# Four token tiles per PSUM bank in the opening of a transformer block, and a weight sum formed from another operand

## The chip, the cores and the metric

The kernel runs on one core of a Trainium2 chip. The metric is the device time of one execution in microseconds. A core has five engines that run side by side, each with its own queue in order: TensorE (PE, matrix products; the loading of its weights is shown as PEld), VectorE (DVE), ScalarE (ACT), GpSimd (POOL) and SyncE (SP, which here only issues transfers). The engines work on SBUF, a memory of 128 partitions. TensorE writes to PSUM, eight banks of 128 x 512 float32 numbers; VectorE and ScalarE read them from there.

## The reference: what is computed

One encoder block over 1024 tokens of width 1024, all in float32:

```python
h = layer_norm(x, ln_in_g, ln_in_b)
proj = h @ w_in[l]                       # 1024 x 11776: q, k, v of three attention groups, HGRN2 inputs, gates
att = dilated_attention(aq, ak, av, slopes)
rec = hgrn2(hq, hf_fwd, hf_bwd, hi, hg, lower_bounds[:, l], hgrn_norm_g[l])
merged = sigmoid(ga) * (att @ w_att_up[l]) + sigmoid(gh) * (rec @ w_hgrn_up[l])
h = layer_norm(ALPHA * h + merged @ w_o[l], ln1_g[l], ln1_b[l])
gate, up = split(h @ w_ffn_in[l], 2)
h = layer_norm(ALPHA * h + (silu(gate) * up) @ w_ffn_out[l], ln2_g[l], ln2_b[l])
```

The change touches the first two lines: the layer norm of `x`, and the way in which `h` and `w_in` are brought into the form in which the large product reads them.

## The kernel before

**Three products for one.** Every float32 operand is split into a high part, rounded to the format `float32r` that TensorE multiplies, and a low part, the rest (`split`, lines 212 and 220: a cast on ScalarE, a subtraction on GpSimd or VectorE). `mm3` (lines 268 to 270) then issues high times high, high times low, and low times high.

**Seven block products instead of eight.** The projection is done by a Strassen-Winograd scheme. The tokens are halved (512 and 512), the 1024 features are halved (512 and 512), and the columns of `w_in` are taken in pairs of tiles of 128. So the transposed activations form four blocks of 512 features by 512 tokens: b11 and b21 (first 512 tokens, lower and upper features) and b12 and b22 (second 512 tokens). From them come t1 = b12 - b11, t2 = b22 - t1, t3 = b22 - b12, t4 = b21 - t2. The seven products read b11, b21, t1, t2, t3, b22 and t4. On the weights' side stand a11, a12, a21, a22 and the sums s1 = a21 + a22, s2 = s1 - a11, s3 = a11 - a21, s4 = a12 - s2.

**The order of products.** `stream` is a generator. It takes two pairs of column tiles (g = 0 and 1) for each group n, and within a group the products in the order 1 (b11), 2 (b21), 6 (t2), 5 (t1), 7 (t3), 3 (b22), 4 (t4), each for both g. For the first two groups products 1 and 2 come ahead of everything else, so that TensorE has work that needs only b11 and b21. One product is four feature blocks of 128, three matmuls each: 12 matmuls of 128 x 512. The weight sums (`sums`, lines 605 to 607 and 610) are emitted five products ahead, the splits of the weights three ahead.

**The opening.** `phase0` makes the seven activation blocks, and calls `run()` to let `stream` emit one more step in between. For each of eight token tiles (128 tokens) it loads `x`, takes mean and variance on VectorE (`stats`, 336 and 340) with three small GpSimd operations (341 to 343), normalises in place on ScalarE in two halves (`norm`, 347), and transposes 128 x 128 squares on TensorE into a PSUM bank with tag `sd` (`transposed`, line 300). In a bank lie four feature blocks of one token tile. Since the gain `g` and the offset `b` of the layer norm differ from feature to feature and features are partitions after the transpose, each 128 x 128 square is evicted by an operation of its own with its own scalars (310 on ScalarE, 312 on VectorE). Tiles 0 to 3 give b11 and b21; tiles 4 to 7 give b12 and b22, and per tile t1 (422), t2 (426), t3 (428, GpSimd) and t4 (429), each 128 x 512 and split by `put`.

**What sets the order.** The program text gives priorities; a planner lays out each engine's queue by them and by its own estimate of when operands are there. Manual dependencies fix the rest: `ordered` chains operations with one key, `behind` puts an operation after a named one. Loads of `x` and of the weights share one chain on SP. There are four PSUM banks with the tag `sd`; the transposes of the opening and the accumulators of product 2 of the first two groups use them.

Of the kernel before, what the change touches and what calls it, by code (L numbers as in the profile page):

```python
# [10 lines left out]
F32 = mybir.dt.float32  # L11
# [68 lines left out]
class Block:  # L80
# [129 lines left out]
    def split(self, hi, lo, src, eng_hi="act", eng_lo="pool", key=None):  # L210
        nc = self.nc
        ins = nc.scalar.copy(hi, src) if eng_hi == "act" else nc.vector.tensor_copy(hi, src)  # L212
        if key == "x":
            self.ordered("xhi", ins)
        elif key == "w":
            self.behind(ins, self.gates.pop(0))
            key = None
# [75 lines left out]
    def transposed(self, pool, n, q, g, b, v=None, bufs=2, on_act=(1, 3, 6), two=False, gate=None):  # L293
# [3 lines left out]
        pa = self.ps_sd() if two else ps  # L297
        for k in range(4):
            p = pa if 4 * q + k in on_act else ps
            ins = nc.tensor.transpose(p[:, 128 * k:128 * (k + 1)], n[:, 128 * (4 * q + k):128 * (4 * q + k + 1)],  # L300
                                      self.ident)
            if gate:
                self.behind(ins, gate)
        if v is None:
            v = pool.tile([128, 4, 128], F32, name="tsv", tag="tsv", bufs=bufs)
        for k in range(4):
            kk = 4 * q + k
            p = (pa if kk in on_act else ps)[:, 128 * k:128 * (k + 1)]
# [5 lines left out]

    def phase0(self, pool, work):


        nc = self.nc
        xs, v, at = [], {}, {}

        def hold(n):
            t = pool.tile([128, D], F32, name=n, tag="xt", bufs=6)
            return t, [t[:, HALF * i:HALF * (i + 1)].rearrange("p (k c) -> p k c", k=4) for i in range(2)]

        def load(n):
            for _ in range(n):
                tt = len(xs)
                xs.append(hold("xt"))
                for h in range(2 if tt == 0 else 1):
                    s = slice(HALF * h, HALF * (h + 1)) if tt == 0 else slice(0, D)  # L330
                    self.queued(xs[tt][0][:, s], self.x[128 * tt:128 * (tt + 1), s])

        def stats(tt):
            st = self.tiny.tile([128, 2, 6], F32, name="bn0", tag="bnst", bufs=3)
            for j in range(2):
                ins = nc.vector.bn_stats(st[:, j, :], xs[tt][0][:, HALF * j:HALF * (j + 1)])
                if tt > 3:
                    self.behind(ins, at["lo", 3, "b11" if tt < 6 else "b21"])
            mv = self.mv0[:, tt, :]
            nc.vector.bn_aggr(mv[:, 0:2], st)  # L340
# [4 lines left out]
        def norm(tt, q):  # L345
            x, mv = xs[tt][0][:, HALF * q:HALF * (q + 1)], self.mv0[:, tt, :]
            ins = nc.scalar.activation(x, x, AF.Identity, bias=mv[:, 3:4], scale=mv[:, 2:3])
            at["norm", tt, q] = ins.ins.name
            if tt > 5:
                self.behind(ins, at["hi", tt - 2, "t2"])  # L350
            elif (tt, q) == (3, 1):
                self.behind(ins, at["hi", 3, "b11"])

        def put(tt, name, src, lo="dve"):
            c = slice(128 * (tt % 4), 128 * (tt % 4) + 128)
            hi, low = self.xb[name]
            ins = self.split(hi[:, :, c], low[:, :, c], src, eng_lo=lo, key="x" if tt > 3 else None)
            at["hi", tt, name], at["lo", tt, name] = self.cast, ins.ins.name
            return ins

        def turn(tt, q, dst, act, gate=None):
            gc, bc = self.col["gin"], self.col["bin"]
            return self.transposed(pool, xs[tt][0], q, gc, bc, dst, on_act=[4 * q + k for k in act], two=len(act) == 2,
                                   gate=gate)

        ACT, DVE = range(4), ()
# [5 lines left out]
        def late(tt, i):  # L372
            put(tt, ("t1", "t3", "b22", "t4")[i], v[tt][i])

# [3 lines left out]
        run(2)  # L378
        load(2)
        run()  # L380
        for tt in range(4):
            v[tt] = self.half3("v11"), self.half3("v21") if tt == 0 else                 pool.tile([128, 4, 128], F32, name=f"v21{tt}")
# [3 lines left out]
        norm(0, 0)  # L386
        norm(0, 1)
        turn(0, 0, v[0][0], DVE)
        stats(1)
        put(0, "b11", v[0][0], "pool")  # L390
        norm(1, 0)
        stats(2)
        turn(1, 0, v[1][0], ACT)
        norm(2, 0)
        put(1, "b11", v[1][0])
        stats(3)
        turn(2, 0, v[2][0], DVE)
        put(2, "b11", v[2][0])
        norm(3, 0)
        turn(3, 0, v[3][0], (2, 3))  # L400
        put(3, "b11", v[3][0])
        self.gates = [at["hi", 1, "b11"]] * 2 + [at["hi", 3, "b11"]] * 2
        run(2)
        for tt in range(4):
            if tt < 3:
                norm(tt + 1, 1)
            turn(tt, 1, v[tt][1], DVE if tt % 2 else ACT, self.product)
            self.left(put(tt, "b21", v[tt][1]))
            if tt == 1:
                load(2)  # L410
                run()
                stats(4)
        self.rest()
        run(3)
        for tt in range(4, 8):
            b11, b21 = v[tt - 4]
            norm(tt, 0)
            norm(tt, 1)
            t1, t2 = xs[tt][1]
            _, (b12, b22) = hold("vt")  # L420
            turn(tt, 0, b12, DVE if tt % 2 else ACT)
            nc.vector.tensor_sub(t1, b12, b11)
            if tt < 7:
                stats(tt + 1)
            turn(tt, 1, b22, ACT if tt % 2 else DVE)
# [1424 lines left out]
```

## Time and profile before

| | us |
|---|---|
| median of three runs | 2102.98 (2100.78 to 2104.03) |
| profiled execution, its time | 2102.44 |
| profiled execution, span of the trace | 2100.6 |
| TensorE busy in the span | 2025.1 |
| VectorE busy | 1380.4 |
| GpSimd busy | 1093.8 |
| ScalarE busy | 931.8 |

The profile shows one execution. Times in a timeline count from the start of the span. In a group of instructions `out<-in` names the tiles that are written and read; behind the first bar stand the busy time of the group in us and the mean of one in ns, behind the second the idle time of the engine ahead of the group and what ended it. `x4` says that the row stands for four instructions. In a row of waits stand the time in total, the number of waits and the longest one. The time of an execution is 1.84 us more than the span of its trace.

### The profile page before, as it was taken

The numbers are of one execution on the slowest core, as the hardware profiler recorded it, in microseconds if no ns is written. First come the engines' busy times: TensorE is split into PE (matmuls) and PEld (weight loads), VectorE is DVE, ScalarE is ACT, GpSimd is POOL, SyncE is SP. The second block draws the span as 40 slices with busy tenths as digits, with TensorE's granted clock in tenths as the row PEclk, the third lists the DMA queues.
The fourth block names the chain that finished last, engine by engine and source line by source line (L and its number), as shares of the span: only waits on it lengthen the run. The fifth ranks groups of instructions, "written<-read, shape, count | busy, mean of one in ns | idle before, by whom it ended". The sixth has DMA issues, their size and how long they took to land.

```text
span 2100.6 us, 30922 instructions
## 1 busy us (share of the span) xinstructions
PE 2025.1 (96%) x10974; PEld 1675.0 (80%) x10974; DVE 1380.4 (66%) x2158; ACT 931.8 (44%) x1878; POOL 1093.8 (52%) x903
## 2 busy tenths in 40 slices
PE   6799999999999999999999899999999999999998
PEld 4588788888887888887888788888788888887876
DVE  7777645885468854788444722347867777767777
ACT  6544455444554436543365531144433333334542
POOL 6476654576446763565635854244666666630012
PEclk9899999999999999999999999999999999999999
DMA  4343442435333353343534764344434344347423
GB/s 146 111 145 111 152 136 94 143 131 161 125 132 113 118 169 109 111 131 121 163 106 157 267 213 150 100 141 135 157 124 147 131 148 133 121 158 288 160 91 125
DMA packets 274845, 297.95 MB, mean 142 GB/s; under 512 B 14018, under 2 KB 207363, under 8 KB 274691
## 3 DMA queue, kind: packets, MB, share of 16 engines
q1 hardware_dynamic: 268384, 274.78, 40.5%
q10 hardware_dynamic: 6306, 21.20, 2.6%
q8 instruction: 86, 1.41, 0.3%
q14 instruction: 69, 0.56, 0.1%
HBM read 201.29 MB, written 94.63 MB: 141 GB/s over the span
## 4 chain that ended last, share of the span: by engine, by line
PE 79%; DVE 9%; issue 5%; POOL 3%; DMA 3%; ACT 1%; SPq 0%; ACTq 0%; DVEq 0%; POOLq 0%
PE pj L268 17%; PE pj L270 17%; PE pj L269 17%; PE sd L269 6%; PE sd L268 6%; PE sd L270 6%; PE sd L1164 2%; POOL w_lo L220 2%; DVE qd L1079 1%; PE sd L920 1%; PE sd L969 1%; PE sd L996 1%; PE sd L1113 1%; DVE hR L1125 1%; PE sd L696 1%
## 5 line engine op out<-in xcount | busy, mean ns | idle before, releaser
L220 POOL TENSOR_TENSOR w_lo<-wa,w_hi 128x512 fp32r<-128x512 f32 x272 | 377.1, 1394 | 290.6 <-ACT w_hi L212 258.9
L212 ACT CAST w_hi<-wa 128x512 fp32r<-128x512 f32 x272 | 167.6, 619 | 249.9 <-PE pj L269 142.9
L220 POOL TENSOR_TENSOR w_lo<-wsum,w_hi 128x512 fp32r<-128x512 f32 x88 | 126.3, 1444 | 113.6 <-PE sd L270 57.5
L220 POOL TENSOR_TENSOR w_lo<-f_raw,w_hi 128x512 fp32r<-128x512 f32 x66 | 102.1, 1554 | 55.7 <-ACT w_hi L212 54.5
L208 POOL TENSOR_TENSOR mv<-mv,mhalf 128x1 f32<-128x1 f32 x16 | 10.8, 679 | 208.2 <-DVE mv L207 208.0
L212 ACT CAST w_hi<-wsum 128x512 fp32r<-128x512 f32 x88 | 54.7, 622 | 126.1 <-PE sd L269 117.7
L268 PE MATMUL pj<-xt1hi,w_hi 128*128 128x512 f32 x252 | 100.6, 399 | 4.9 <-ACT wkeep L633 2.7
L268 PE MATMUL pj<-xb22hi,w_hi 128*128 128x512 f32 x252 | 99.3, 394 | 0.0
L270 PE MATMUL pj<-xb22hi,w_lo 128*128 128x512 f32 x252 | 98.4, 391 | 0.8 <-POOL w_lo L220 0.8
L269 PE MATMUL pj<-xt1lo,w_hi 128*128 128x512 f32 x252 | 99.1, 393 | 0.0
L270 PE MATMUL pj<-xt1hi,w_lo 128*128 128x512 f32 x252 | 98.8, 393 | 0.0
L269 PE MATMUL pj<-xb22lo,w_hi 128*128 128x512 f32 x252 | 98.3, 390 | 0.0
L220 POOL TENSOR_TENSOR w_lo<-ws,w_hi 128x512 fp32r<-128x512 f32 x46 | 64.8, 1414 | 56.0 <-ACT w_hi L212 53.2
L212 ACT CAST gwsum<-a_raw 128x512 fp32r<-128x512 f32 (+1 forms) x78 | 47.7, 616 | 101.4 <-PE pj L269 46.3
L633 ACT COPY wkeep<-pj 128x512 f32<-128x512 f32 x136 | 79.3, 583 | 28.8 <-DVE evh L511 13.3
L268 PE MATMUL pj<-xt2hi,w_hi 128*128 128x512 f32 x192 | 78.6, 410 | 10.8 <-ACT xt2hi L212 10.8
L484 DVE TENSOR_TENSOR evh<-wkeep,pj 128x512 f32<-128x512 f32 x66 | 57.6, 880 | 44.3 <-PE pj L270 29.7
L606 POOL TENSOR_TENSOR wa<-wa,wa 128x512 f32<-128x512 f32 x46 | 69.4, 1517 | 31.2 <-DVE ws L605 28.5
L220 DVE TENSOR_TENSOR gwkeep<-a_raw,gwsum 128x512 fp32r<-128x512 f32 (+1 forms) x78 | 57.7, 739 | 41.9 <-ACT gwsum L212 39.0
L495 DVE TENSOR_TENSOR evh<-wkeep,pj 128x512 f32<-128x512 f32 x45 | 30.6, 683 | 78.7 <-PE pj L270 59.0
L268 PE MATMUL pj<-xb11hi,w_hi 128*128 128x512 f32 x192 | 77.3, 405 | 3.4 <-ACT xb11hi L212 2.3
L1116 ACT ACTIVATE hS<-hR,dec 128x128 f32<-128x128 f32 x112 | 44.4, 402 | 76.7 <-DVE hR L1125 46.9
(418 smaller groups left out, 6659.7 us busy)
## 6 DMA issues: line engine op xcount, KB each, us to landing
wa<-in_w_in_dram SPq DMA_DIRECT2D x184, 256.0 KB, 3.3
f_raw<-in_w_ffn_in_dram SPq DMA_DIRECT2D x44, 512.0 KB, 4.0
a_raw<-gd SPq DMA_DIRECT2D x30, 512.0 KB, 3.6
gd<-fc SPq DMA_DIRECT2D x44, 256.0 KB, 2.0
gd<-fs SPq DMA_DIRECT2D x33, 256.0 KB, 2.1
tg<-evh SPq DMA_DIRECT2D x32, 256.0 KB, 3.1
tg<-tg SPq DMA_DIRECT2D x16, 512.0 KB, 3.5
y<-ahs SPq DMA_DIRECT2D x16, 512.0 KB, 4.9
```

The source lines that it names most:

```text
L212: ins = nc.scalar.copy(hi, src) if eng_hi == "act" else nc.vector.tensor_copy(hi, src)
L220: ins = e.tensor_sub(lo, src, hi.bitcast(F32))
L268: nc.tensor.matmul(ps, whi, xhi, start=first, stop=False, **kw)
L269: nc.tensor.matmul(ps, whi, xlo, start=False, stop=False, **kw)
L270: self.product = nc.tensor.matmul(ps, wlo, xhi, start=False, stop=last, **kw).ins.name
L484: self.left(nc.vector.tensor_tensor(o, self.order_src(add, g, kind), s, OP.add))
L495: self.left(nc.vector.tensor_add(t, add, ps))
L606: nc.gpsimd.tensor_sub(a["a21"], a["a11"], a["a21"])
L633: nc.scalar.copy(t, ps)
L696: nc.tensor.transpose(ps[:, 128 * k:128 * (k + 1)], cols(4 * b + k), self.ident)
L1116: nc.scalar.activation(S[:, c, :], E, AF.Copy, scale=dec[:, 1, c:c + 1])
L1164: nc.tensor.matmul(po[:, jj, :], l, r, start=(n == 0), stop=(n == len(terms) - 1))
```

## The change

In the opening one bank now holds one feature block of four token tiles (512 tokens) instead of four feature blocks of one tile. So one operation with one scalar per partition evicts 128 x 512. The gain is applied while a bank is read (`scaled`); the offset is added where the high and the low part are made (`hi`, `lo`), or cancels: t1 is made directly from PSUM as g times the bank minus the scaled b11 (`less`), a value z2 for t2 in the same way, and t3 gets the difference of the two offsets. The intermediate values lie in memory lent from activation blocks that are filled later. t4's subtraction moves from VectorE to GpSimd. The loads of token tiles 4 to 6 stand further ahead in SP's chain. On ScalarE and on VectorE the operations up to b21 are chained by hand. In `sums` the second sum comes ahead of the third, which reads a22 and the second sum.

```diff
+        def turn(tt, q, ks=range(4)):
+            for k in ks:
+                if tt % 4 == 0:
+                    banks[k] = self.ps_sd()
+                nc.tensor.transpose(banks[k][:, 128 * (tt % 4):128 * (tt % 4) + 128],
+                                    xs[tt][:, 128 * (4 * q + k):128 * (4 * q + k) + 128], self.ident)
+        def scaled(w, k, q, on_act):
+            g = column("gin", 4 * q + k)
+            if on_act:
+                act(w[k], banks[k], AF.Copy, scale=g)
+            else:
+                dve(nc.vector.tensor_scalar(w[k], banks[k], g, None, op0=OP.mult))
+        def less(o, k, q, w):
+            dve(nc.vector.scalar_tensor_tensor(o[k], banks[k], column("gin", 4 * q + k), w[k], op0=OP.mult,
+                                               op1=OP.subtract))
+        def hi(name, k, src, b=None):
+            z = self.xb[name][0][:, k, :]
+            return act(z, src[k], AF.Copy if b is None else AF.Identity, **({} if b is None else {"bias": b}))
+        def lo(name, k, src, b=None):
+            h, z = (t[:, k, :] for t in self.xb[name])
+            if b is None:
+                return dve(nc.vector.tensor_sub(z, src[k], h.bitcast(F32)))
+            return dve(nc.vector.scalar_tensor_tensor(z, src[k], b, h.bitcast(F32), op0=OP.add, op1=OP.subtract))
...
         load(4)
         next(cols)
-        run(2)
+        run()
         load(2)
         run()
+        load()
+        run()
         stats(0)
...
+        for tt in range(4):
+            norm(tt, 0)
+            turn(tt, 0)
+            if tt < 3:
+                stats(tt + 1)
+                norm(tt, 1)
...
+        norm(3, 1)
+        stats(4)
+        self.gates = [None] * 2 + [h.ins.name] * 2
         run(2)
+        load()
         for tt in range(4):
+            turn(tt, 1)
+        for k in range(4):
+            scaled(w21, k, 1, k % 2 == 0)
+        for k in range(4):
+            hi("b21", k, w21, bias[1][k])
+            self.left(lo("b21", k, w21, bias[1][k]))
...
+        for k in (0, 2):
             for tt in range(4, 8):
+                turn(tt, 0, (k, k + 1))
+            for i in (k, k + 1):
+                less(t1, i, 0, w11)
             run()
+        for k in (0, 2):
+            for tt in range(4, 8):
+                turn(tt, 1, (k, k + 1))
+            for i in (k, k + 1):
+                less(z2, i, 1, t1)
+            for i in (k, k + 1):
+                h = hi("t2", i, z2, bias[1][i]), lo("t2", i, z2, bias[1][i])
+                scaled(w22, i, 1, True)
+            run()
+        for k in range(4):
+            nc.gpsimd.tensor_sub(w11[k], z2[k], w11[k])
+        for k in range(4):
+            self.behind(hi("t1", k, t1), h[0].ins.name)
+            self.behind(lo("t1", k, t1), h[1].ins.name)
...
                 if p == 6:
                     self.behind(nc.vector.tensor_add(a["s1"], a["a21"], a["a22"]))
-                    nc.gpsimd.tensor_sub(a["a21"], a["a11"], a["a21"])
                     nc.vector.tensor_sub(a["a11"], a["s1"], a["a11"])
+                    nc.gpsimd.tensor_sub(a["a21"], a["a22"], a["a11"])
                     a["s3"], a["s2"] = a["a21"], a["a11"]
```

More of the change, by code (lines that the diff above doesn't have):

```diff
@@ L215, in split @@
         elif key == "w":
-            self.behind(ins, self.gates.pop(0))
+            last = self.gates.pop(0)
+            if last:
+                self.behind(ins, last)
             key = None
@@ L345, in norm @@
         def norm(tt, q):
[L346 to L366, printed above, removed]
+            x, mv = xs[tt][:, HALF * q:HALF * (q + 1)], self.mv0[:, tt, :]
+            return act(x, x, AF.Identity, bias=mv[:, 3:4], scale=mv[:, 2:3])
+        def turn(tt, q, ks=range(4)):
[4 more added lines that the diff above has]
+                                    xs[tt][:, 128 * (4 * q + k):128 * (4 * q + k) + 128], self.ident)
@@ L440, in phase0 @@
+        for k in range(4):
+            hi("b22", k, w22, bias[1][k])
+            lo("b22", k, w22, bias[1][k])
+        run()
+        for k in range(4):
+            nc.gpsimd.tensor_sub(w21[k], w21[k], z2[k])
+        self.forms("t4")
+        for k in range(4):
+            hi("t4", k, w21)
+            lo("t4", k, w21)
         for _ in cols:
```

126 lines of the change are left out of this document (54 added, 72 removed).

## The prediction

> **What bounds the kernel now.** First the page's head, to see which engine is full. TensorE is busy in 96% of the span, so only its gaps can be won.
>
> ```profile
> span 2100.6 us, 30922 instructions
> PE 2025.1 (96%) x10974; PEld 1675.0 (80%) x10974; DVE 1380.4 (66%) x2158; ACT 931.8 (44%) x1878; POOL 1093.8 (52%) x903
> ```
>
> Then the busy time by stage, cut at the points where TensorE's work changes (columns: length, busy time and instructions of PE, PEld, DVE, ACT, POOL, granted clock, DMA share, GB/s):
>
> ```profile
> 0.00:19.48 19.48, 4.71 (x17) 3.04 (x17) 11.36 (x27) 11.77 (x21) 9.68 (x28) 1.00 0.88 276
> 19.48:34.50 15.02, 14.86 (x64) 11.57 (x64) 8.38 (x18) 11.26 (x23) 8.55 (x11) 1.00 0.50 146
> 34.50:54.10 19.60, 15.94 (x73) 12.56 (x72) 19.57 (x31) 11.51 (x25) 16.99 (x15) 0.91 0.04 15
> 54.10:68.94 14.84, 1.56 (x8) 0.95 (x8) 14.25 (x24) 7.41 (x17) 4.61 (x4) 0.61 0.27 88
> 68.94:77.64 8.70, 8.29 (x25) 6.24 (x26) 8.70 (x14) 8.42 (x17) 1.29 (x2) 0.68 0.00 0
> 77.64:200.00 122.36, 121.66 (x650) 101.24 (x649) 86.58 (x111) 54.77 (x103) 86.88 (x77) 1.00 0.41 132
> ```
>
> From 77.64 us on TensorE is full (121.66 of 122.36). Before it lie two holes: 0 to 19.48, and 54.10 to 68.94, where VectorE is busy 14.25 of 14.84. I call the products of the opening P0 to P9, 12 matmuls each: P0 to P3 multiply b11, P4 to P7 b21, P8 and P9 the token sum t2. The waits of TensorE up to 78 us, and the ends of its work:
>
> ```profile
> PE pj L268 <- ACT xt2hi L212: 10.8, 1, 10.8
> PE sd L300 <- ACT xt L347: 8.0, 5, 2.4
> ...
> 31.41 0.39 PE L270 MATMUL pj<-xb11hi,w_lo 128*128 128x512 f32 x1
> 34.13 0.39 PE L270 MATMUL pj<-xb11hi,w_lo 128*128 128x512 f32 x1
> 71.16 0.63 PE L270 MATMUL pj<-xt2hi,w_lo 128*128 128x512 f32 x1
> 72.44 0.63 PE L270 MATMUL pj<-xt2hi,w_lo 128*128 128x512 f32 x1
> 77.25 0.39 PE L270 MATMUL pj<-xt2hi,w_lo 128*128 128x512 f32 x1
> ```
>
> P8 waits for t2; P9 ends at 77.25 + 0.39 = 77.64. Warm, 12 matmuls take 34.13 - 31.41 = 2.72 us, 0.227 each; after the hole three take 1.28, 0.43 each. So the forecast is one number: where P9 ends afterwards. All that follows is TensorE's own work and shifts with it.
>
> **The change, part by part.**
>
> *VectorE in the opening.* Its groups from 14.50 to 71.72 us, the last operand of t2 and a little more, and the sum of that stretch:
>
> ```profile
> 14.50:71.72 57.22, 35.85 (x153) 27.25 (x154) 48.67 (x81) 37.91 (x78) 33.53 (x31) 0.85 0.30 95
> ...
> L429 DVE TENSOR_TENSOR v<-v,xt 128x512 f32<-128x512 f32 x4 | 6.7, 1670 | 0.1
> L312 DVE TENSOR_SCALAR vt<-sd,vc 128x128 f32<-128x128 f32 x16 | 5.5, 397 | 0.1
> L336 DVE BATCH_NORM_STATS2 bn<-xt 128x6 f32<-128x512 f32 x8 | 4.9, 672 | 0.0
> L312 DVE TENSOR_SCALAR v<-sd,vc 128x128 f32<-128x128 f32 x13 | 4.5, 404 | 4.2 <-PE sd L300 4.2
> L426 DVE TENSOR_TENSOR xt<-vt,xt 128x512 f32<-128x512 f32 x4 | 3.5, 877 | 0.2
> L422 DVE TENSOR_TENSOR xt<-vt,v 128x512 f32<-128x512 f32 x4 | 3.4, 856 | 0.2 <-ACT vt L310 0.2
> L220 DVE TENSOR_TENSOR xt2lo<-xt,xt2hi 128x512 fp32r<-128x512 f32 x4 | 2.7, 678 | 0.0
> L495 DVE TENSOR_TENSOR evh<-wkeep,sd 128x512 f32<-128x512 f32 x2 | 1.3, 673 | 0.0
> L511 DVE SCALAR_TENSOR_TENSOR evh<-evh,wkeep 128x512 f32<-128x512 f32 x2 | 1.3, 677 | 0.0
> L340 DVE BATCH_NORM_AGGREGATE mv<-bn 128x2 f32<-128x12 f32 x4 | 0.7, 196 | 0.0
> ```
>
> A 128x128 eviction costs 0.40 us, a 128x512 read of PSUM 0.67 (L495): one operation instead of four saves 0.9. Removed here: 29 small evictions (10.0 us), the L429 subtractions (6.7, to GpSimd), and L422 and L426 (6.9), whose work is now done while reading PSUM. Afterwards VectorE must do, up to t2's last low half: 4 scalings out of PSUM (0.67: 2.7), 8 subtractions out of PSUM for t1 and t2 (0.67: 5.4), 12 low halves of b11, b21, t2 with the offset inside (taken as L511, 0.68: 8.2), the statistics of tiles 4 to 7 (8 x 0.672 + 4 x 0.2: 6.2), four weight sums (0.68: 2.7), six operations that evict P4 to P7 (0.675: 4.0). Sum 29.2 us undisturbed, against 48.67 busy now.
>
> Undisturbed is too kind. L429 took 1.67 us, L220 with the same shapes 0.68. The timeline shows what ran beside it:
>
> ```profile
> 61.69 1.77 POOL L428 TENSOR_TENSOR vt<-vt 128x512 f32<-128x512 f32 x1 [4.10 <-DVE xt L422]
> 62.37 1.64 DVE L429 TENSOR_TENSOR v<-v,xt 128x512 f32<-128x512 f32 x1
> ```
>
> So an operation with two SBUF inputs beside a GpSimd tensor operation costs about 1 us more. Sixteen of the new operations have two SBUF inputs (12 low halves, 4 sums). Bounds: none disturbed, 0; all, 16 x 0.97 = 15.5. GpSimd is busy 33.53 of 57.22, so I take half: 7.8. VectorE's work is then 37.0.
>
> The Trainium skill ("SBUF — State Buffer", "SBUF: two separate sides") calls the port pair that VectorE and GpSimd share an exclusive lock: the later instruction waits for the whole of the earlier. The pair above agrees: VectorE's started inside GpSimd's 1.77 us and ended 0.55 after it. By that rule an operation that meets the start of GpSimd's waits 1.77, and half of sixteen would cost 14.2 instead of 7.8: P9's end 6.4 later than below and a time near 2088, which is the first rival.
>
> *The start of P0.*
>
> ```profile
> 10.41 1.23 DVE L336 BATCH_NORM_STATS2 bn<-xt 128x6 f32<-128x512 f32 x2
> 11.56 1.35 DVE L312 TENSOR_SCALAR v<-sd,vc 128x128 f32<-128x128 f32 x4
> 12.82 0.20 DVE L340 BATCH_NORM_AGGREGATE mv<-bn 128x2 f32<-128x12 f32 x1
> 14.09 0.27 POOL L343 TENSOR_SCALAR mv<-mv 128x1 f32<-128x1 f32 x1
> 15.21 0.80 ACT L347 ACTIVATE xt<-xt,mv 128x512 f32<-128x512 f32 x1
> 16.07 1.11 PE L300 MATMUL sd<-tabs_sb,xt 128*128 128x128 f32 x4 [2.19 <-ACT xt L347]
> 18.81 0.62 ACT L212 CAST xb11hi<-v 128x512 fp32r<-128x512 f32 x1
> 28.25 1.03 PE L300 MATMUL sd<-tabs_sb,xt 128*128 128x128 f32 x8
> ```
>
> Without the evictions between, tile 3's aggregate comes 1.2 us earlier, at 11.6. GpSimd's three small operations end 1.54 after its start (14.36 - 12.82), near 13.2, and the normalisation (0.80) near 14.0; four cold transposes take 1.1, the first bank is whole at 14.4, and a scaling (0.67 at most) and a cast (0.62) give the first operand near 16.0, against 19.48. The rest follows one feature block at a time, each 128x512 wide.
>
> *Loads.* Tiles 4 and 5 (1.05 MB) go ahead of the first weights of the second quadruple.
>
> ```profile
> 10.00:20.00 10.00, 3.86 (x13) 2.65 (x14) 7.79 (x18) 9.49 (x19) 6.07 (x11) 1.00 1.05 303
> 19.34 1.14 ACT L212 CAST w_hi<-wfirst 128x512 fp32r<-128x512 f32 x2
> ```
>
> At 303 GB/s those weights land 3.5 us later. They are cast only after b11's last cast (19.34 now, near 18.5 then), and P2, their user, starts after P0 and P1, near 22.5: hidden. Without that cover it would be 3.5. The eighth tile's load waits for tile 0's second half to be transposed, which I put near 17, and the two loads left for P6 and P7 stand behind it; P6 starts after 35, so nothing waits.
>
> *TensorE's floor.* From 16.0: 120 matmuls (27.2), 48 transposes by L300's eight in 1.03 (6.2), some 15 cold matmuls at 0.2 more (3.0): P9 cannot end before 52.4.
>
> The Trainium skill ("TensorE: Matmul & The Clock Gate", Part 1) lets the clock halve after some 3.4 us of idling and return after as long a busy stretch; an estimate by it is 16 cold matmuls per long hole, 3.2 us. The trace agrees: the granted clock is 0.61 in the hole and 0.68 after it.
>
> *The sum.* VectorE starts on b11 at 14.9. With 37.0 of work it ends at 51.9; of its present 8.55 us idle in that stretch I keep 3 (it still waits for b21's transposes): 54.9. Behind t2's last low half TensorE has 6 to 15 matmuls of P8 and P9 left, 1.4 to 3.4 us; I take 2.1: P9 ends at 57.0. That is 77.64 - 57.0 = 20.6 us less.
>
> *What is late next.* t1's low halves (4 x 0.68) stand behind t2's, inside P8 and P9 (5.4). GpSimd makes t3 (4 x 1.77 at most, 7.1), with two products more of cover. t4, also new on it, comes 10.9 us later still. Each costs nothing unless GpSimd's weight splits stand ahead; I put 0 to 3 on it, and as much on stalls moved about later. ScalarE loses 30 small evictions for 8 wide ones: not the bound.
>
> *Third weight sum.* It leaves the path of the second sum and stands behind it, in all 46 pairs of column tiles.
>
> ```profile
> L607 DVE TENSOR_TENSOR wa<-ws,wa 128x512 f32<-128x512 f32 x46 | 60.4, 1319 | 17.7 <-POOL wa L606 15.8 <-POOL w_lo L220 1.9
> PE pj L270 <- POOL w_lo L220: 7.2, 6, 4.3
> ```
>
> VectorE's 15.8 us of waiting goes, but TensorE waited for GpSimd's splits only 7.2 us in the whole run. Bounds: 7.2 won, or as much lost; I take 0, as VectorE is not the bound there.
>
> **The rivals.**
>
> *Ports and banks eat a third.* All 16 operations disturbed: 7.8 more, P9 ends near 65, 2090. The four sd banks lead to the same place: the opening's banks stay open until the eighth tile is normalised, and P4 to P7 each want one too. Three waits of a product's length (8.1) give 2090 also. For it: the waits on L347 (8.0). Against: every bank is now freed by one or two wide reads.
>
> *It does not do what it says.* VectorE stays the bound, with all disturbed and its present idle time: 14.9 + 29.2 + 15.5 + 8.55 + 2.1 = 70.3, 2095; with 3 us lost later, 2098 to 2102.
>
> *Slower.* The third sum behind the second delays the weights of its product in each of the 46 pairs. At a whole L607 (1.32) that is 60.7 us: 2142. It decides from 20.6 / 46 = 0.45 us each. Against it: the sums are made five products (13.6 us) ahead.
>
> **How the numbers follow.** The sum is made against the profiled execution: span 2100.6, time 2102.44, so 2102.44 - 20.6 = 2081.8, 2082; the median of the runs, 2102.98, is 0.5 above. Chances: forecast 0.62 (from TensorE's floor 2077, less 3, to 2088), ports or banks 0.23 (2088 to 2096), not what it says 0.06, slower 0.09. The range 2074 to 2094 takes the first and most of the second. Below 0.2% (4.2 us) a measurement hardly tells a change: faster 0.85, same 0.06, slower 0.09.
>
> **What would show it.** Right: the first matmul near 16, no hole over 4 us before P8, P9's end at 52 to 59, VectorE's groups 128x512 wide. Wrong: that end beyond 65, TensorE waiting for sd banks or for GpSimd's splits after it, or more waits on w_lo between 200 and 1200.

## The result and the profile after

The changed kernel takes 2086.11 us (median of four runs, 2083.05 to 2087.28), the kernel before 2101.88 beside it: a ratio of 0.9929 (95% interval 0.9917 to 0.9942), 15.8 us less. 2082.0 was forecast, in a range of 2074 to 2094. The head of the profile's page of the changed kernel:

```profile
span 2084.2 us, 30889 instructions
PE 2022.3 (97%) x10974; PEld 1672.3 (80%) x10974; DVE 1365.6 (66%) x2125; ACT 928.0 (45%) x1856; POOL 1090.3 (52%) x907
```

The span is 16.4 us shorter than before (2100.6), and TensorE's busy time only 2.8: what went is idle time of TensorE. The busy time by stage of the changed kernel, cut at its own points: the first row ends at the first matmul of a product (16.78), the second runs from the start of P8 (48.19) to the end of P9 (58.86), the fourth is the stream of products after the opening, the last one the stretch in which VectorE makes the operands up to t2.

```profile
0.00:16.78 16.78, 5.91 (x23) 4.23 (x24) 7.62 (x17) 9.38 (x13) 9.26 (x28) 1.00 0.95 297
...
48.19:58.86 10.67, 9.74 (x44) 7.11 (x42) 10.67 (x9) 6.29 (x12) 10.67 (x8) 1.00 0.13 49
58.86:145.00 86.14, 76.28 (x325) 60.14 (x325) 68.85 (x73) 40.58 (x73) 56.88 (x47) 0.96 0.44 141
145.00:1200.00 1055.00, 1034.96 (x6631) 864.64 (x6630) 673.78 (x1256) 519.75 (x1164) 612.87 (x541) 0.99 0.42 138
14.50:57.60 43.10, 39.37 (x168) 30.67 (x168) 35.16 (x46) 30.03 (x50) 30.29 (x31) 0.92 0.32 95
```

The same view of the kernel before, for the two stretches behind P9:

```profile
77.64:145.00 67.36, 66.73 (x301) 54.47 (x300) 50.40 (x57) 30.16 (x54) 51.41 (x43) 1.00 0.51 161
145.00:1200.00 1055.00, 1029.60 (x6590) 858.12 (x6590) 680.32 (x1249) 512.42 (x1153) 611.79 (x537) 0.99 0.42 136
```

The hole ahead of P8 is gone: P8 starts at 48.19 instead of 68.94, and P9 ends 77.64 - 58.86 = 18.8 us earlier. But behind P9 TensorE was idle for 67.36 - 66.73 = 0.6 us before, and is idle for 86.14 - 76.28 = 9.9 now, with a granted clock of 0.96. In the stream it is the other way round: 25.4 us idle before, 20.0 now.

How the lead changes on the way can be read from ScalarE's copies of full banks (`wkeep`), of which there are 204 in both kernels. From the timelines, the 15th and the 135th copy, of the kernel before

```profile
144.02 0.58 ACT L633 COPY wkeep<-pj 128x512 f32<-128x512 f32 x1
1202.91 0.58 ACT L633 COPY wkeep<-pj 128x512 f32<-128x512 f32 x1
```

and of the changed kernel:

```profile
139.31 0.58 ACT L679 COPY wkeep<-pj 128x512 f32<-128x512 f32 x1
1188.02 0.57 ACT L679 COPY wkeep<-pj 128x512 f32<-128x512 f32 x1
```

So of the 18.8 us that P9 is ahead, 4.7 are left at the 15th copy: 14.1 melt within 85 us. From there to the 135th copy the lead grows to 14.9, by 10.2. At the last copy (1867.7 before) it is 15.6, at the end of the span 16.4. The forecast had the opening alone as the source, and all of it kept. TensorE's waits in the changed kernel, up to P9 and from there to 145 us (total, number, longest):

```profile
PE sd L364 <- ACT xt L331: 5.8, 5, 2.6
...
PE sd L364 <- DVE evh L541: 2.0, 1, 2.0
...
PE sd L271 <- DVE xt1lo L390: 3.9, 3, 3.4
PE pj L270 <- DVE evh L541: 3.1, 1, 3.1
PE pj L270 <- ACT w_hi L212: 2.2, 2, 1.5
PE pj L272 <- POOL w_lo L222: 0.4, 1, 0.4
```

The four rows behind P9 make 9.6 of its 9.9 us: t1's low halves, an eviction, a pair of weights. What VectorE and GpSimd do around the first of them, with the first matmul and the end of P9, from the timeline of the changed kernel:

```profile
16.78 1.20 PE L270 MATMUL pj<-xb11hi,w_hi 128*128 128x512 f32 x2
...
47.25 1.75 POOL L481 TENSOR_TENSOR v<-v,lent_xt4lo 128x512 f32<-128x512 f32 x1
47.76 3.48 DVE L391 SCALAR_TENSOR_TENSOR xt2lo<-lent_xt4lo,vc,xt2hi 128x512 fp32r<-128x512 f32 x2
48.94 1.76 POOL L463 TENSOR_TENSOR lent_xb22hi<-lent_xt4lo,lent_xb22hi 128x512 f32<-128x512 f32 x1
...
54.12 3.48 DVE L391 SCALAR_TENSOR_TENSOR xt2lo<-lent_xt4lo,vc,xt2hi 128x512 fp32r<-128x512 f32 x2
57.53 1.77 DVE L390 TENSOR_TENSOR xt1lo<-lent_xt3hi,xt1hi 128x512 fp32r<-128x512 f32 x1
58.46 0.40 PE L272 MATMUL pj<-xt2hi,w_lo 128*128 128x512 f32 x1
59.83 2.85 DVE L656 TENSOR_TENSOR wa<-wa,wa 128x512 f32<-128x512 f32 x2
64.39 0.61 PE L271 MATMUL sd<-xt1lo,w_hi 128*128 128x512 f32 x1 [3.43 <-DVE xt1lo L390]
```

While GpSimd makes t3 (L463) and t4 (L481), t2's low halves take 1.74 us each, t1's first 1.77, and between t1's first and second stand two fourth sums (L656) with 2.85. TensorE waits 3.43 us for t1's second.

So two things had to be found out: what eats the lead of the opening, and whether the gain in the stream is the third weight sum's, which the forecast put at nothing.

### The profile page after: what moved, and what is told of

It is laid out like the page before. It is cut to its first block, busy times and chain, and to the rows that moved or that the text cites. A ratio compares the mean times of both kernels' runs of the same rounds, so it can differ in the third digit from the quotient of the medians.

```text
span 2084.2 us, 30889 instructions
## 1 busy us (share of the span) xinstructions
PE 2022.3 (97%) x10974; PEld 1672.3 (80%) x10974; DVE 1365.6 (66%) x2125; ACT 928.0 (45%) x1856; POOL 1090.3 (52%) x907
## 4 chain that ended last, share of the span: by engine, by line
PE 57%; DVE 6%; issue 2%; DMA 2%; ACT 1%; POOL 0%; SPq 0%; ACTq 0%; DVEq 0%; POOLq 0%
PE pj L271 12%; PE pj L270 12%; PE pj L272 12%; PE sd L271 6%; PE sd L270 6%; PE sd L272 6%; PE sd L1210 1%; DVE qd L1125 1%; DVE a L500 0%; DVE hR L1171 0%; DVE gwkeep L222 0%; PE sd L1015 0%; PE sd L966 0%; DVE hR L1170 0%; DMA w<-in_w_ffn_out_dram 0%
## 5 line engine op out<-in xcount | busy, mean ns | idle before, releaser
L222 POOL TENSOR_TENSOR w_lo<-wa,w_hi 128x512 fp32r<-128x512 f32 x272 | 371.6, 1375 | 285.4 <-ACT w_hi L212 261.1
L222 POOL TENSOR_TENSOR w_lo<-f_raw,w_hi 128x512 fp32r<-128x512 f32 x66 | 102.6, 1563 | 52.4 <-ACT w_hi L212 51.2
L208 POOL TENSOR_TENSOR mv<-mv,mhalf 128x1 f32<-128x1 f32 x16 | 10.7, 678 | 207.3 <-DVE mv L207 207.2
L530 DVE TENSOR_TENSOR evh<-wkeep,pj 128x512 f32<-128x512 f32 x66 | 57.4, 878 | 41.4 <-PE pj L272 29.5
L270 PE MATMUL pj<-xt4hi,w_hi 128*128 128x512 f32 x192 | 77.0, 401 | 3.9 <-DVE evh L541 3.1
L272 PE MATMUL pj<-xt2hi,w_lo 128*128 128x512 f32 x192 | 77.0, 402 | 2.2 <-POOL w_lo L222 2.2
L271 PE MATMUL pj<-xt2lo,w_hi 128*128 128x512 f32 x192 | 77.0, 401 | 0.9 <-DVE xt2lo L391 0.9
```

Of the source, the lines that this page charges most:

```text
L208: nc.gpsimd.tensor_tensor(mv[:, 2:3], mv[:, 2:3], self.mhalf[:, 0:1], OP.pow)
L222: ins = e.tensor_sub(lo, src, hi.bitcast(F32))
L270: nc.tensor.matmul(ps, whi, xhi, start=first, stop=False, **kw)
L271: nc.tensor.matmul(ps, whi, xlo, start=False, stop=False, **kw)
L272: self.product = nc.tensor.matmul(ps, wlo, xhi, start=False, stop=last, **kw).ins.name
L530: self.left(nc.vector.tensor_tensor(o, self.order_src(add, g, kind), s, OP.add))
```

## The experiments

In each, "lead" is by how much the 15th and the 135th copy come earlier than in the kernel before, and the times stand beside runs of that kernel on the same chip. Times are medians; leads, waits and the ends of products are read from the one profiled execution of each kernel.

### Each part alone

The kernel before with the new order of the sums only:

```diff
-                    nc.gpsimd.tensor_sub(a["a21"], a["a11"], a["a21"])
                     nc.vector.tensor_sub(a["a11"], a["s1"], a["a11"])
+                    nc.gpsimd.tensor_sub(a["a21"], a["a22"], a["a11"])
```

> The kernel before with one edit: in the weight sums the second sum comes ahead of the third, which reads a22 and the second sum. My step (the sum is off TensorE's path): 2100 to 2104 us, ratio 0.999 to 1.001. Rival, that this edit won the 8 us by which the changed kernel gains between 200 and 1050 us: 2090 to 2096, ratio 0.995 to 0.997.

And the changed kernel with the old order of the sums (the same three lines the other way round):

> The changed kernel with the weight sums as before (third sum from a11 and a21, ahead of the second). My step: the opening carries the whole gain, 2084 to 2088 us, ratio 0.992 to 0.994. Rival, third sum: only some 5 to 8 us are left of the gain, 2094 to 2098. Both say that P9 ends near 58.9 us.

Measured: the sums alone 2097.31 us, ratio 0.9978 (0.9969 to 0.9987), between the two ranges of the expectation; the opening alone 2096.04, 0.9974 (0.9965 to 0.9983), within the rival's. The leads at the 15th and the 135th copy are -4.9 and +6.3 with the sums alone, +3.8 and +4.9 with the opening alone. So the growth in the stream belongs to the sums: 11.2 us with them, 1.1 without. And the opening alone, though its P9 ends at 61.75 (not near 58.9 as both sides had expected) instead of 77.64, keeps 5 of these 16 us.

The group of the second sum over the whole run, of the kernel with the new sums only (it is L607 in the prediction's row, with the same columns):

```profile
L606 DVE TENSOR_TENSOR wa<-ws,wa 128x512 f32<-128x512 f32 x46 | 39.0, 869 | 5.5 <-POOL w_lo L220 5.3
```

The second sum no longer waits 15.8 us for GpSimd's third, and takes 869 ns instead of 1319: 46 x 0.45 = 20.7 us of VectorE's time, beside the wait. TensorE's idle time from 145 to 1200 us falls from 25.4 to 1055 - 1035.96 = 19.0:

```profile
145.00:1200.00 1055.00, 1035.96 (x6648) 0.99 0.43 138
```

In the kernel before, the longest wait of the whole run for GpSimd's split was 4.3 us, at 1191.80. There the second sum stood behind the third on GpSimd, and the cast and the split of its product behind the second. With the new order the waits for splits from 145 to 1200 us fall from 6.6 to 2.3 us. That is 4.3 of the 6.4 us of idle time gained; the rest is spread over other waits.

The parts don't add: 4.4 and 5.7 us alone, 15.8 together, by the medians. Alone, the new sums lose 4.9 us up to the 15th copy, 1.4 of them ahead of the end of P9 (79.03 instead of 77.64); with the new opening they don't (4.7 with them, 3.8 without). Why was not followed further: the planner's order around the opening differs between these kernels.

### The third sum on VectorE

The other way to take GpSimd out of the second sum's path: the kernel before, third sum in its old place and form, on VectorE.

```diff
-                    nc.gpsimd.tensor_sub(a["a21"], a["a11"], a["a21"])
+                    nc.vector.tensor_sub(a["a21"], a["a11"], a["a21"])
```

> The kernel before with the third weight sum on VectorE, in its old place between the first and the second. Theory, that the 11 us between 145 and 1200 us come from VectorE's wait for GpSimd in the middle of its queue: that wait is gone here too, and from the 15th to the last copy of the stream 6 to 12 us are won, time 2091 to 2098. Rival, that GpSimd beside VectorE was what cost (the second sum 1.32 us each, 0.91 afterwards): the second sum falls to about 0.9 here too, but 46 more sums on VectorE take back 31 us of its time, and the time is 2098 to 2106.

Measured: 2095.1 us, ratio 0.9976 (0.9963 to 0.9989); leads of -3.3 and +6.1. So 9.4 us are gained in the stream, nearly as with the new order (11.2), though the third sum reads the old operands; the time is the theory's, not the rival's. So it is not the other formula that pays, but what the two kernels have in common: the second sum no longer waits for GpSimd.

### Two orders and one buffer in the opening

What melts the lead? First the order: t4's subtractions on GpSimd put behind t3's last low half on VectorE, so that fewer of them run beside t2 and t1.

```diff
-            lo("t3", k, w11, diff[:, k:k + 1])
+            done = lo("t3", k, w11, diff[:, k:k + 1])
...
-            nc.gpsimd.tensor_sub(w21[k], w21[k], z2[k])
+            self.behind(nc.gpsimd.tensor_sub(w21[k], w21[k], z2[k]), done.ins.name)
```

> The changed kernel, with GpSimd's four subtractions for t4 put behind t3's last low half. Theory, that GpSimd's new work slowed the low halves of t1 and so opened the 3.4 us hole after P9: the three low halves of t1 fall from 1.8 us each to below 1, TensorE's waits for them from 3.9 us to below 2, and product 11 ends 2 to 5 us earlier; the time falls to 2082 to 2084. Rival, that what is won there is lost again in the burst of VectorE work at 90 to 118 us: the same hole shrinks, but the time stays at 2085 to 2087.

Measured: 2083.0 us, ratio 0.9914 (0.9900 to 0.9927); leads of 8.2 and 21.0. This is the time of the theory, but the interval overlaps the changed kernel's, and the mechanism is not the one expected. `behind` orders the plan, but here, between two engines, it made nobody wait at run time: GpSimd ran t4's subtractions from 60.72, while t3's first low half starts at 66.97:

```profile
60.72 6.21 POOL L481 TENSOR_TENSOR v<-v,lent_xt4lo 128x512 f32<-128x512 f32 x4
```

So they lie beside t1's low halves, which take 1486 ns on average against 1489 in the changed kernel, not below 1 us as expected, and TensorE waits 2.6 us for them instead of 3.9; t2's fall from 1779 to 1513. P9 ends at 57.06 instead of 58.86, the second product on t1 (the next pair behind P9) at 67.21 instead of 70.72. Of these 3.5 us, 1.9 lie ahead of P8, which starts at 46.30 instead of 48.19. The stretch from the start of P6 to that of P8, of the changed kernel and of this one:

```profile
38.91:48.19 9.28, 9.28 (x36) 7.46 (x37) 5.73 (x8) 3.67 (x7) 6.32 (x6) 0.72 0.08 30
37.88:46.30 8.42, 8.42 (x37) 6.91 (x37) 5.69 (x8) 3.64 (x6) 6.14 (x6) 0.80 0.09 33
```

TensorE is full in both; 0.9 us of the difference is the granted clock, 0.80 instead of 0.72. So what this order of GpSimd is worth is not shown by its total.

Then the fourth sums behind t1's last low half:

```diff
-            self.behind(lo("t1", k, t1), h[1].ins.name)
+            done = lo("t1", k, t1)
+            self.behind(done, h[1].ins.name)
+        self.left(done)
```

> The changed kernel, with VectorE's two fourth sums (2.85 us beside GpSimd's work, now between the first and the second low half of t1) put behind t1's last low half. Theory, VectorE's order opens the hole: the wait of 3.4 us for t1's low half falls below 1, product 11 ends 2 to 3.5 us earlier, and as TensorE is full behind it the time falls by as much, to 2083 to 2084. Rival, what is won is lost again behind product 11: 2085 to 2087.

Measured: 2083.02 us, 0.9918 (0.9899 to 0.9936); leads of 8.8 and 19.6. TensorE's waits for t1's low halves shrink from 3.9 to 1.7 us, and t1's pair ends at 68.43, 2.3 earlier; P9 is where it was (59.24). This interval overlaps the changed kernel's too. Both edits together:

> Both: t4's subtractions on GpSimd behind t3's last low half, and the fourth sums behind t1's last low half. If the two parts of the hole add up: TensorE's wait for t1's low half below 0.7 us, product 11 ends 5 to 6 us earlier than in the changed kernel, time 2080 to 2082. If they are the same part: as with the first alone, 2083.

Measured: 2082.83 us, 0.9919 (0.9897 to 0.9941), leads of 7.9 and 18.3. Not better than each alone, though t1's pair ends at 65.62, 5.1 earlier: TensorE's waits behind P9 move on to the next low halves and to an eviction.

```profile
PE pj L271 <- DVE xt3lo L391: 2.5, 2, 1.8
PE pj L270 <- DVE evh L543: 1.7, 1, 1.7
```

The waits for weights at 87.7 and 90.0 us I put down to lent memory: `w22` lies in what becomes t4's high part, so the cast of t4 waits for b22's last low half, and ScalarE's next casts of weights stand behind it. With two buffers of its own for `w22`:

```diff
-        w11, t1, w22, z2 = (lent(z) for z in ("xb22hi", "xt3hi", "xt4hi", "xt4lo"))
+        w11, t1, z2 = (lent(z) for z in ("xb22hi", "xt3hi", "xt4lo"))
...
+        own = [pool.tile([128, D], F32, name="w22", tag="xt", bufs=7) for _ in range(2)]
+        w22 = [own[k // 2][:, HALF * (k % 2):HALF * (k % 2) + HALF] for k in range(4)]
```

> The changed kernel, with the scaled b22 in two token buffers that are free by then instead of in the memory lent from t4's high part. Theory, that t4's casts wait for b22's low halves only because of the lent memory, and hold up the weights behind them on ScalarE: the waits of 0.7 and 1.5 us on w_hi at 87 to 90 us go, the time falls by 1.5 to 3 us, to 2083 to 2085. Rival, the burst of VectorE work: the waits go, the time stays at 2085 to 2087.

Measured: 2089.14 us, 0.9946 (0.9933 to 0.9960), leads of 1.3 and 9.8 (its profiled execution was the slowest of four, 2094.4). The waits on `w_hi` shrink from 2.2 to 0.7 us, but that on the eviction grows from 3.1 to 3.7 and one of 1.5 on `w_lo` comes: this theory fell. In the changed kernel's trace, too, the cast ahead of the wait at 90.0 had been released by VectorE's second sum, not by a low half of b22. The lead is gone elsewhere when those waits go: P8 already starts 1.8 us later (50.02). And the growth in the stream, with the same sums, is 8.5 us here, 10.2 in the changed kernel, 12.8 with t4 late. So a few us differ between these kernels for no reason that I can name (the planner's order, the clock), and single waits of 1 or 2 us cannot be told by the total.

### Without GpSimd's subtractions

The eight subtractions that make t3 and t4 are left out, so that t3 and t4 hold other values; everything else is issued as before.

```diff
-        for k in range(4):
-            nc.gpsimd.tensor_sub(w11[k], z2[k], w11[k])
...
-        for k in range(4):
-            nc.gpsimd.tensor_sub(w21[k], w21[k], z2[k])
```

> The changed kernel without GpSimd's eight subtractions that make t3 and t4 (left out, so t3 and t4 hold other values; everything else runs). Theory, the shared path of VectorE and GpSimd: the low halves of t2 and t1, 1.74 and 1.45 us now, fall to 0.7 to 0.8, P9 ends 3 to 5 us earlier, at 54 to 56, and the hole behind it closes below 1 us. Rival, these operations are slow for another reason (the offset inside, the memory lent): they stay above 1.3 us, and P9 at 58 to 59.

Measured, one run: 2077.64 us, a span of 2075.9, 8.3 less than the changed kernel's; leads of 13.2 and 23.4. VectorE's group of t2's low halves in the kernel without the subtractions (14.50 to 57 us):

```profile
L391 DVE SCALAR_TENSOR_TENSOR xt2lo<-lent_xt4lo,vc,xt2hi 128x512 fp32r<-128x512 f32 x4 | 3.0, 748 | 0.1
```

The end of its P9, from its timeline:

```profile
56.12 0.39 PE L272 MATMUL pj<-xt2hi,w_lo 128*128 128x512 f32 x1
```

And the groups of low halves in the changed kernel (14.50 to 57.60 us), with GpSimd's two groups of subtractions (45 to 61 us):

```profile
L391 DVE SCALAR_TENSOR_TENSOR xt2lo<-lent_xt4lo,vc,xt2hi 128x512 fp32r<-128x512 f32 x4 | 7.0, 1779 | 0.0
L391 DVE SCALAR_TENSOR_TENSOR xb21lo<-v,vc,xb21hi 128x512 fp32r<-128x512 f32 x4 | 3.8, 959 | 2.6 <-ACT xb21hi L331 2.6
...
L481 POOL TENSOR_TENSOR v<-v,lent_xt4lo 128x512 f32<-128x512 f32 x4 | 7.0, 1740 | 0.0
L463 POOL TENSOR_TENSOR lent_xb22hi<-lent_xt4lo,lent_xb22hi 128x512 f32<-128x512 f32 x4 | 6.5, 1631 | 0.0
```

748 ns against 1779, with no other change to that operation: t2's four low halves cost 4.0 us more for the subtractions beside them. P9 ends at 56.12 + 0.39 = 56.5 without them, 2.4 earlier (3 to 5 were expected), and t1's pair at 62.38 instead of 70.72, 8.3 earlier; that is the whole difference of the spans. Only 0.6 of it lies ahead of P8 (47.60 instead of 48.19): from P8's start to the end of t1's pair are 14.8 us instead of 22.5, with the same order of operations on VectorE. So these 13.5 us of GpSimd, which the forecast let lie beside other work, are paid in VectorE's time. VectorE loses more at t2; TensorE waits more at t1, which VectorE reaches later. t1's low halves still take 1230 ns, not 0.7 to 0.8 us, since GpSimd's splits of weights run beside two of them.

### The subtractions on VectorE

If the cost lies in the two engines stretching each other, VectorE itself can do the eight subtractions more cheaply: t3's behind t1's last low half, t4's behind t3's, with the fourth sums late as above.

```diff
-            nc.gpsimd.tensor_sub(w11[k], z2[k], w11[k])
+            self.behind(hi("t1", k, t1), h[0].ins.name)
+            done = lo("t1", k, t1)
+            self.behind(done, h[1].ins.name)
         for k in range(4):
-            self.behind(hi("t1", k, t1), h[0].ins.name)
-            self.behind(lo("t1", k, t1), h[1].ins.name)
+            self.behind(nc.vector.tensor_sub(w11[k], z2[k], w11[k]), done.ins.name)
+        self.left(done)
...
-            lo("t3", k, w11, diff[:, k:k + 1])
+            gone = lo("t3", k, w11, diff[:, k:k + 1])
...
-            nc.gpsimd.tensor_sub(w21[k], w21[k], z2[k])
+            self.behind(nc.vector.tensor_sub(w21[k], w21[k], z2[k]), gone.ins.name)
```

> The eight subtractions that make t3 and t4 go from GpSimd to VectorE, t3's behind t1's last low half and t4's behind t3's, with the fourth sums behind t1's low halves too, as in the run before that moved these alone. Theory (GpSimd's subtractions cost because VectorE's two-input operations in SBUF stretch while they run; without them P9 ended at 56.5 and the run was 2077.6): t2's low halves take 0.7 to 0.8 us each instead of 1.74, P9 ends at 56 to 58, and the end is 2077 to 2081 us, since the eight operations that VectorE takes over are 8 x 0.7 = 5.6 us, most of them beside t1's twelve-matmul products. Rival (it was not the stretching but the work itself, which now lies on the engine that bounds the opening): the first matmul on t3 waits 3 us or more and the end is 2083 us or later.

Measured: 2079.63 us (2077.89 to 2083.02), ratio 0.9903 (0.9888 to 0.9917), by the medians the fastest kernel here that computes everything. P9 ends at 55.01 (56 to 58 were expected), t1's pair at 60.88; leads of 14.5 and 23.7. From the timeline of this kernel:

```profile
48.85 1.56 DVE L391 SCALAR_TENSOR_TENSOR xt2lo<-lent_xt4lo,vc,xt2hi 128x512 fp32r<-128x512 f32 x2
...
54.94 4.69 DVE L467 TENSOR_TENSOR lent_xb22hi<-lent_xt4lo,lent_xb22hi 128x512 f32<-128x512 f32 x4
```

Two low halves of t2 take 1.56 us instead of 3.48. t3's subtractions take 4.69, more than the 4 x 0.7 of the expectation, since GpSimd splits weights beside two of them (1.78 each); even so TensorE waits only 0.39 us for t3. The work was not dearer on the engine that bounds the opening; the rival (2083 or later) fell. Beside the run with only the fourth sums moved its span is 3.9 us shorter; the intervals of the two ratios overlap.

Not all of that is the subtractions' either: from the start of P6 to that of P8 the clock stayed full in this execution,

```profile
39.28:46.10 6.82, 6.82 (x36) 5.74 (x37) 5.62 (x9) 3.63 (x6) 4.21 (x4) 1.00 0.16 57
```

behind the same two waits of TensorE (2.02 and 0.98 us) that the kernel without the subtractions has (2.03 and 0.99), where the same stretch took 8.43 us at 0.80. So the stretch to compare is the one behind the start of P8, where the subtractions are:

| kernel | P8 starts | P9 ends | t1's pair ends | P8's start to there |
|---|---|---|---|---|
| changed | 48.19 | 58.86 | 70.72 | 22.5 |
| t4 late | 46.30 | 57.06 | 67.21 | 20.9 |
| fourth sums late | 48.41 | 59.24 | 68.43 | 20.0 |
| both | 47.65 | 58.35 | 65.62 | 18.0 |
| without the subtractions | 47.60 | 56.51 | 62.38 | 14.8 |
| subtractions on VectorE | 46.10 | 55.01 | 60.88 | 14.8 |

Done by VectorE, the subtractions cost TensorE nothing up to there, and done by GpSimd 7.7 us; the two orders win back part of it.

Last, the same with the third sum on VectorE too:

```diff
-                    nc.gpsimd.tensor_sub(a["a21"], a["a22"], a["a11"])
+                    nc.vector.tensor_sub(a["a21"], a["a22"], a["a11"])
```

> The same, and the third weight sum (from a22, behind the second) goes to VectorE too. Theory (the third sum's worth in the stream is that VectorE and GpSimd no longer hold each other up, and GpSimd is free for w_lo): the stream from 200 to 1200 us loses 1 to 4 us more, from waits on w_lo that were 3.9 us in the changed kernel, and the end is 2074 to 2079 us. Rival (VectorE has no room for 46 more operations of 0.7 us in the stream): waits on VectorE's evictions grow by more than those on w_lo shrink, and the end is the same as with the subtractions alone or later.

Measured: 2086.67 us, 0.9938 (0.9923 to 0.9953); leads of 10.7 and 14.8. My theory fell here: it is 7.0 us slower by the medians (8.6 by the spans), 3.8 lost ahead of the 15th copy and 5.1 in the stream. The first part is lost ahead of P8, which starts at 50.08 instead of 46.10 (TensorE waits 2.35 us for `less` instead of 0.98, and the clock behind it is 0.82); from there to the end of t1's pair are 14.8 us again. The stream's stage of this kernel (all engines):

```profile
145.00:1200.00 1055.00, 1027.49 (x6601) 857.67 (x6600) 697.93 (x1283) 515.00 (x1153) 558.19 (x500) 1.00 0.42 137
```

TensorE's waits in it:

```profile
PE sd L1189 <- DVE hR L1172: 9.3, 4, 2.7
PE pj L270 <- DVE evh L532: 3.6, 2, 2.2
PE sd L1145 <- POOL t L1128: 2.4, 1, 2.4
```

The same stage of the kernel with the subtractions alone on VectorE:

```profile
145.00:1200.00 1055.00, 1036.80 (x6623) 865.61 (x6623) 668.69 (x1243) 516.54 (x1155) 612.07 (x540) 0.99 0.43 139
```

And TensorE's waits there:

```profile
PE sd L1189 <- DVE hR L1172: 7.7, 4, 2.7
...
PE pj L272 <- POOL w_lo L222: 2.2, 3, 1.0
PE pj L270 <- DVE evh L532: 1.9, 2, 1.4
```

VectorE is 29 us busier in the stream, and TensorE's idle time rises from 18.2 to 27.5: it waits longer for the HGRN states (`hR`), evictions (`evh`) and the HGRN's `t`. (That is 9.3 us more idle time where the lead loses 5.1; I did not follow the rest.) The waits on `w_lo`, which this was to remove, were 2.2 us. Once the second sum waits for nobody, GpSimd's time costs TensorE less than VectorE's.

## Why the prediction was right, and where its steps were not

The time came out 4 us above the forecast, but not by the forecast's sum. That was -20.6 us from the opening and 0 from everything else. The measured sum is -18.8 at P9, +14.1 up to the 15th copy, -10.2 from there to the 135th, -0.7 to the last copy and -0.8 at the end: -16.4 in the span. Two errors of more than 10 us each stand against each other. That the total came out so near is luck: the opening alone, the only source that the forecast counted, takes 2096.04 us, outside its range. Right was the mechanism up to P9; wrong was what follows it, and the third sum.

*VectorE's sum* held in its main part. The work from 14.50 to 57.60 us is 35.16 us, against 37.0. Disturbed were t2's four low halves (mean 1779 ns) and three or four of the other twelve operations, near the half of 16 that was taken, and by 1779 - 748 = 1.03 us each, the 1 us that was taken. Idle time was mis-sized: 43.10 - 35.16 = 7.9 us, not 3; VectorE waited 2.6 for the high parts of b21 and 4.2 and 3.6 for TensorE (the rest of these lies ahead of 14.50). The 3.6 were for P6, whose matmuls came 0.43 us apart, at half clock; the forecast had cold matmuls in TensorE's floor only, not in VectorE's waits. Where the clock stayed full (the subtractions on VectorE), this wait is 1.1. So t2's last low half ended at 57.60 instead of 54.9, and the tail behind it was 1.3 us instead of 2.1: P9 at 58.86, not 57.0.

*The start of P0* was 16.78, near 16.0. The loads cost nothing that shows: the DMA share was 0.95 up to the first matmul, and no wait of TensorE up to P9 names a load of weights or tokens.

*TensorE's floor* stood: the best P9 of all runs is 55.01, above 52.4.

*"All that follows is TensorE's own work and shifts with it"* failed, and with it the claim that the forecast is one number. Behind P9 TensorE was fully fed before because the other engines had worked ahead during the hole. When P9 ended, at 77.64, VectorE had made the low halves of t1, t3 and b22 and begun t4's, from the timeline of the kernel before:

```profile
76.46 2.49 DVE L220 TENSOR_TENSOR xt4lo<-v,xt4hi 128x512 fp32r<-128x512 f32 x4
```

In the changed kernel none of these was finished when P9 ended (58.86; t1's first was under way), and t4's first starts at 76.74. VectorE had also made six weight sums before, four now; of GpSimd's splits 12 were finished before and 11 now. So what had been made ahead were operands from the tokens, and hardly weights. With the hole gone, the next late operand of each engine shows: t1's low halves, weights, an eviction, 9.9 us where 0.6 had been, and a clock of 0.96. Even without t3's and t4's subtractions the lead falls from 21.1 at P9 (77.64 - 56.5) to 13.2, and the longest waits there are for GpSimd's splits:

```profile
PE pj L272 <- POOL w_lo L222: 4.9, 2, 2.9
```

*"What is late next"* named the right operands at the wrong price. t1's low halves were taken as 4 x 0.68 inside P8 and P9. They took 1.77 and then 4.03 for the other three, with 2.85 of fourth sums between. GpSimd's subtractions for t3 and t4, "each costs nothing", with 0 to 3 us put on both, cost 7.7 from P8 to the end of t1's pair, not by being late themselves but by what they do to VectorE's operations beside them. The prediction had priced this for the sixteen operations up to t2 and not for the four of t1 and the fourth sums behind them.

*The third weight sum* was taken at 0, between bounds of 7.2 either way. It was worth 9 to 11 us in the stream (11.2 alone, 10.2 less 1.1 beside the new opening), beyond the bound. The bound came from TensorE's waits on GpSimd's splits alone (7.2). But the second sum also held VectorE for 15.8 us of waiting and ran 0.4 us longer each time, and what queued behind it on VectorE came later; that this is how it reached TensorE is inferred, no run isolates it. The argument "VectorE is not the bound there" (64% busy) looked at the share of busy time, where it should have asked what stands behind a waiting instruction. Of the 10.2 us, 5.4 are TensorE's idle time (25.4 to 20.0); some 15 fewer matmuls at half clock at 0.2 each make about 3 more; the remaining 2 I can't assign.

*The slower rival* (the third sum delays its product's weights) has no sign: the waits on `w_lo` in the stream fell from 6.6 to 3.9 us. *Ports and banks:* the lower price of the two was right up to t2. A lasting block by sd banks does not show: the wait for an eviction of an sd bank (`PE sd L364 <- DVE evh`) is 2.0 us, once.

The Trainium skill's rule of an exclusive lock ("SBUF — State Buffer", "SBUF: two separate sides") was weighed in the prediction with a wait of 1.77 us for each disturbed operation, P9 at 63.4 and a time near 2088. The trace has 1.03 us more for each, and P9 at 58.86; that 2088 lies near the 2086.11 measured is chance, since the lead was lost behind P9 and not ahead of it. What the rule says of taking turns agrees in the main with the pace shown at the end of this document.

## What to carry to other kernels

A stall that is removed was also the time in which other engines worked ahead: before you let all that follows "shift", ask for each engine what it made during the stall, and who waits for it once there is none. A GpSimd operation moved "beside other work" is not free where VectorE has two SBUF operands at the same time; price it in VectorE's stretched operations, and try it on VectorE itself. A dependency that only orders the plan does not hold an engine back at run time: look in the trace where the operation ran. Compare two kernels stage by stage, since a different clock ahead of a stage can look like the worth of an edit in it. And price a wait of an engine that is not the bound by what is queued behind the waiting instruction, not by its busy share.

## What the runs showed of the hardware

**Two engines in step.** In the changed kernel VectorE's low halves of t2 and GpSimd's subtractions go in step: two operations of VectorE in 3.48 us, GpSimd's starting at 47.25 and 48.94, 1.69 apart. Without the subtractions VectorE's took 0.75. GpSimd's subtraction took 1.29 where it started first (at 46.01); the operation with two SBUF inputs that VectorE began beside it at 46.31 took 1.53, against 0.68 in the kernel without the subtractions. One of each in about 1.7 us is little less than one behind the other (2.04), so not much is won by running them side by side. `less` (L380), which reads one of its operands from PSUM, kept its 0.7 us in the same stretch.

**A late drop of the clock.** After the hole of 3.14 us that ended at 117.75, the first matmuls came 0.23 us apart, at the full clock; those from 119.6 to 122.2 came 0.43 apart; after that they were fast again. From the timeline of the changed kernel:

```profile
117.75 0.47 PE L270 MATMUL pj<-xt4hi,w_hi 128*128 128x512 f32 x1 [3.14 <-DVE evh L541]
...
120.02 0.63 PE L272 MATMUL pj<-xt4hi,w_lo 128*128 128x512 f32 x1
120.45 0.63 PE L270 MATMUL pj<-xt4hi,w_hi 128*128 128x512 f32 x1
```

So here half clock did not come at once: it began some 1.5 us after the hole, while TensorE was busy again, and lasted 3.4 us. The Trainium skill ("TensorE: Matmul & The Clock Gate", Part 1) has the clock halve after an idle window of about 3.4 us; here 3.14 were enough, and the drop came after the hole, both of which I had not expected. Nor do 3 us mark a threshold: ahead of P6 the changed kernel has waits of 2.02 and 0.53 us with 1.43 us of transposes between, and P6 ran at half clock (0.50 from 38 to 44 us), while in the kernel with the subtractions on VectorE waits of 2.02 and 0.98 us in the same place were followed by full clock, as was the hole of 1.54 us at 90.0. The length of a hole alone does not tell whether the clock drops.

**Reciprocals.** The hole of 3.14 us was a wait for an eviction queued behind four reciprocals of the HGRN, from the timeline of VectorE in the changed kernel:

```profile
109.28 3.35 DVE L1125 RECIPROCAL qd<-fa 128x256 f32<-128x256 f32 x2
112.56 3.30 DVE L1128 RECIPROCAL qd<-fb 128x256 f32<-128x256 f32 x2
...
116.93 0.67 DVE L541 TENSOR_TENSOR evh<-wkeep,pj 128x512 f32<-128x512 f32 x1
```

A reciprocal of 128x256 took 1.66 us, two and a half times an eviction of 128x512 (0.67), and four stood in a row: 6.5 us (109.28 to 115.78) in which VectorE freed no bank.
